# Attention on one core: pair 1's keys and queries loaded in halves, two more output pairs stored whole

## The chip, the cores and the metric

The kernel runs on one NeuronCore of one Trainium2 chip. TensorE (PE in the profile) multiplies matrices and transposes, ScalarE (ACT) computes the exponentials, VectorE (DVE) and GpSimd (POOL) do the elementwise work, and SyncE (SP) issues nearly all transfers between device memory and the on-chip memory SBUF. Sixteen DMA engines carry every transfer. The metric is the device time of one execution in microseconds (us). The kernel before takes 114.5 us, the median of three runs from 113.86 to 114.7.

## The reference

Attention over 64 independent heads (8 batches of 8), each with 512 rows of 64 numbers:

```
scores = einsum('bhqd,bhkd->bhqk', q, k) * (1 / sqrt(64))
scores = scores - scores.max(axis=-1, keepdims=True)
attn = exp(scores);  attn = attn / attn.sum(axis=-1, keepdims=True)
out = einsum('bhqk,bhkd->bhqd', attn, v)        # all float32, (8, 8, 512, 64)
```

Each of q, k, v and the output is 8 MB. A head of one of them is 128 KB. The kernel works on fp16 copies, subtracts one constant instead of each row's maximum, and gets the sum of a row from a column of ones beside the values.

## The kernel before

**Tiling.** The 64 heads are taken as 32 pairs, numbered 0 to 31, each with a head 0 and a head 1. (g,h) below is head h of pair g. A row of the SBUF tile of one pair holds four rows of each head, so that one partition reads 1 KB in one piece from each head.

**The way of one pair.** Its k, q and v are loaded in one transfer of 256 KB each (`load`, L488), cast to fp16 (`cast`: keys and queries at L504, values at L494, all on GpSimd; for queries of pair 1 alone VectorE casts one half at L502 and GpSimd the other at L503). Eight transposes on TensorE (L535) and a copy on VectorE (L548; for pair 1 two copies at L542) give the layout that the scores need. Score matmuls (L575) fill a PSUM tile of 128x1024, and ScalarE takes its exponential in one instruction (L579). For 16 of the tiles VectorE computes the exponential with bit operations instead (L599 and L616 to L639), which gives two tiles, pe and pd, that the value matmuls (L680) add up. The first pair has code of its own (`first_pair`, L729), with its k and q loaded head by head, on two queues (L722, L723).

**Output.** A unit is 128 query rows of one head; four units make a head. VectorE normalises up to seven units at once (reciprocal L645, product L650) into a ring of 112 units, and `store` sends a head, 128 KB, to memory (L670). Heads are numbered in the ring in the order in which their values are computed, from unit 4 on; (8,0) has units 68 to 71, (8,1) 72 to 75, (10,0) 84 to 87, (10,1) 88 to 91. The first product writes three units, 4 to 6, and product number n + 1 writes units 7n to 7n + 6, so unit u is overwritten by the product that writes unit u + 112, which has to wait until the store of unit u has landed. For the pairs in `PAIRED` (3 and 13) head 0's turn issues nothing, and head 1's turn issues one transfer of 256 KB for both (L668).

**Order.** A planner (`Plan`) walks through an estimated time line before the kernel is built and writes one list of steps. Every engine gets its instructions in the order of this list; semaphores make each wait for its data. The list does not depend on `PAIRED`. First SP issues the first pair's q, then 21 loads in this order: keys 1, queries 1, keys 2, queries 2, values 0, keys and queries 3, keys and queries 4, keys and queries 5, values 1, and so on to keys and queries 7. Keys, queries and values each have seven buffers, so the loads of later pairs wait for casts of earlier ones. Late in the list, loads and stores alternate on SP's queue. Around the change it reads: stores (6,0), (6,1); keys and queries 29; stores (8,0), (8,1); keys and queries 30; values 28 and 26; store (9,0); keys and queries 31; stores (9,1), (10,0); values 29 and 27; stores (10,1), (11,0).

**Waits of transfers.** Each transfer reports its end on one of eight semaphores, taken in turn by all queues. A transfer is issued when the one that had its semaphore before, eight places earlier, has landed.

Of the kernel before, what the change touches and what calls it, by code (L numbers as in the profile page):

```python
# [17 lines left out]
class Plan:  # L18
# [25 lines left out]
    SCALE_PORT, PRODUCT_PORT, GAP, REACH = 271, 537, 20, 5  # L44
    FIRST_LAND, LOAD, STORE, LATENCY, ISSUE = 5200, 740, 370, 2300, 470
    QUEUED, URGENT = 3500, 16
    PAIRED = (3, 13)
    RAW, QK16, NV, NU = 7, 5, 12, 112
    PAIR, DUEK, DUEV, DUEL, PRE = 3300, 2800, 4000, 7000, 0

# [357 lines left out]
def kernel(  # L408
# [7 lines left out]
    nc = tc.nc  # L416
# [50 lines left out]
    def source(src, g):  # L467
        b, h = g // ppb, 2 * (g % ppb)
        return src[b, h : h + 2].rearrange("h (p i) d -> p h i d", i=NI)

    def load_tile(g, name):
        t = lpool.tile(
            [P, 2, NI, D],
            FP32,
            tag=f"{name}32",
            name=f"{name}32_{g}",
            bufs=7,
        )
        raw.setdefault(g, {})[name] = t
        return t  # L480

    def load(g, names):
        if g >= NP:
            return
        for name in names:
            src = {"q": q, "k": k, "v": v}[name]
            t = load_tile(g, name)
            nc.sync.dma_start(out=t[:, :, :, :], in_=source(src, g))  # L488

    def cast(g, name):  # L490
# [167 lines left out]
    def store():  # L658
# [4 lines left out]
        u = u0 % NU  # L663
        if g in Plan.PAIRED and h == 0:
            return
        if g in Plan.PAIRED:
            both = ring[:, u - NI : u + NI, :].rearrange("p (h i) d -> p h i d", h=2)
# [149 lines left out]
    with tc.manual_schedule():  # L817
        plan = Plan(groups, NP, 3)
        steps = plan.run()
        first_loads()  # L820
        for g, name in plan.first_loads:
            load(g, name)
        make_identity(nc, ident)
        for n in range(NV):
            nc.vector.memset(vps[n][:, :, :, D : D + 1], 1.0)
        first_pair()
        do = {
            "transposes": transposes,
            "scores": scores,
            "values": values,  # L830
            "load": load,
            "store": store,
            "cast": cast_behind,
            "raise": raise_,
            "copy": lambda g, b: copy(g),
            "pass": pass_,
            "last": last_values,
            "finish": finish,
            "rec": lambda u, n, b: reciprocal(u, n),
            "mul": lambda u, n, b: normalise(u, n),  # L840
        }
        for what, *args in steps:
            do[what](*args)
# [30 lines left out]
```

## Time and profile before

| | us |
|---|---|
| median of three runs | 114.5 (113.86 to 114.7) |
| profiled execution, whole | 114.31 |
| its span, first to last instruction | 112.5 |
| TensorE busy | 104.0 |
| VectorE busy | 101.3 |
| ScalarE busy | 105.6 |
| GpSimd busy | 65.2 |

In one line of the groups stand the line of the kernel, the engine, the operation, what is written from what, the shapes and the count; behind the first bar the busy time and the mean duration of one in ns; behind the second the idle time of the engine ahead of these instructions and what ended it. A line of the timeline has the start in us, the duration in us, the engine and what it does; in brackets stands the idle time before it. Instructions that follow one another are merged, with their count. SPq is SP's queue of transfers. A line of the transfers has the size of one and the median time from issue to landing. A line of a table of windows has the stretch, its length, the busy time of each engine with its count, TensorE's granted clock, the share of time in which the DMA engines were busy, and GB/s. The share can be a little over 1, since packets overlap.

### The profile page before, as it was taken

Reading aid. Unit: us, or ns where it says so; the run is one execution under the profiler, and the core shown is the slowest. Engines: PE = TensorE matmul, PEld = TensorE weight load, DVE = VectorE, ACT = ScalarE, POOL = GpSimd, SP = SyncE. Lnnn points to the kernel's source line nnn. Section 1 sums busy time; section 2 is a strip of 40 time slices with the busy share of each in tenths; the row PEclk is TensorE's granted clock in tenths of the full one; section 3 lists DMA queues with packets and bytes.
Section 4 is the critical chain, followed back from the end, with each engine's and each line's share of the span. In section 5 each row is a group of like instructions: output and inputs, shape, how many; then the busy total and the mean of one; then the engine's idle time right before and its main releaser. Section 6 shows DMA issues by size and latency. Waiting matters only on the chain.

```text
span 112.5 us, 4427 instructions
## 1 busy us (share of the span) xinstructions
PE 104.0 (92%) x1731; PEld 71.1 (63%) x1731; DVE 101.3 (90%) x226; ACT 105.6 (94%) x118; POOL 65.2 (58%) x127
## 2 busy tenths in 40 slices
PE   7988889899999998999999999999999999999970
PEld 7654546576775564657677557678667765776560
DVE  1547999999989999999999999999999999999760
ACT  4689999999999999999999999999999999999960
POOL 2166788265478866686847888755868796000000
PEclk9999999999999999999999999999999999999999
DMA  2999999999999999999999999999997976848435
GB/s 90 271 340 354 346 349 349 342 349 348 348 329 331 344 350 347 344 353 325 283 299 376 346 312 363 358 374 353 357 305 229 289 244 212 270 143 268 159 99 184
DMA packets 35349, 33.84 MB, mean 301 GB/s; under 512 B 2560, under 2 KB 35328, under 8 KB 35328
## 3 DMA queue, kind: packets, MB, share of 16 engines
q1 hardware_dynamic: 34752, 33.04, 90.8%
q10 hardware_dynamic: 576, 0.52, 1.4%
q8 instruction: 13, 0.21, 0.8%
q14 instruction: 8, 0.07, 0.2%
HBM read 25.17 MB, written 8.39 MB: 298 GB/s over the span
## 4 chain that ended last, share of the span: by engine, by line
DVE 45%; PE 42%; ACT 7%; issue 2%; DMA 1%
PE o L680 18%; PE st L575 14%; DVE pd L599 10%; DVE tqk L548 8%; DVE ring L650 8%; ACT pt L579 7%; PE tp L535 6%; DVE m L633 4%; DVE pd L639 3%; PE st_0a L727 3%; DVE pe L625 3%; DVE m L616 2%; DVE m L635 2%; DVE rc L645 2%; DMA out_dram<-ring 1%
## 5 line engine op out<-in xcount | busy, mean ns | idle before, releaser
L579 ACT ACTIVATE pt<-st 128x1024 f16<-128x1024 f32 (+1 forms) x110 | 100.3, 1114 | 0.0
L680 PEld LDWEIGHTS <-pt 128*128 128x128 f16 x880 | 38.9, 98 | 12.3 <-issue 10.6
L680 PE MATMUL o<-vp,pt 128*128 128x65 f16 x880 | 46.3, 194 | 0.2
L575 PE MATMUL st<-tqk 64*128 64x512 f16 (+1 forms) x250 | 42.4, 381 | 2.9 <-ACT pt L579 1.7
L504 POOL CAST qkp<-k 128x512 f16<-128x512 f32 x31 | 21.5, 692 | 12.2 <-DMA k<-in_k_dram 5.2
L494 POOL CAST vp<-v 128x512 f16<-128x512 f32 x32 | 21.8, 695 | 7.7 <-DVE rc L645 2.6
L504 POOL CAST qkp<-q 128x512 f16<-128x512 f32 x30 | 21.1, 703 | 6.6 <-DVE rc L645 2.2
L650 DVE TENSOR_TENSOR ring<-o,rc 128x448 f32<-128x448 f32 (+2 forms) x37 | 22.3, 606 | 0.6
L680 PE MATMUL o<-vp,pe 128*128 128x65 f16 x128 | 22.1, 195 | 0.0
L680 PE MATMUL o<-vp,pd 128*128 128x65 f16 x128 | 21.9, 193 | 0.0
L548 DVE COPY tqk<-tp 128x1024 f16<-128x1024 f16 x30 | 20.3, 677 | 0.2 <-PE tp L535 0.2
L535 PE MATMUL tp<-ident,qkp 128*128 128x128 f16 x248 | 19.5, 219 | 0.9 <-DVE ring L650 0.7
L599 DVE TENSOR_SCALAR pd<-st 128x1024 uint16<-128x1024 f32 x16 | 19.5, 1217 | 0.7 <-PE st L575 0.7
L575 PEld LDWEIGHTS <-tqk 64*128 64x128 f16 x250 | 11.7, 93 | 12.3 <-issue 4.8
L535 PEld LDWEIGHTS <-qkp 128*128 128x128 f16 x248 | 14.3, 97 | 7.3 <-issue 4.4
L680 PEld LDWEIGHTS <-pe 128*128 128x128 f16 x128 | 12.5, 97 | 3.8 <-issue 2.9
L680 PEld LDWEIGHTS <-pd 128*128 128x128 f16 x128 | 12.5, 98 | 0.0
L639 DVE TENSOR_TENSOR pd<-pd,m 128x1024 f16<-128x1024 f16 x16 | 10.9, 682 | 0.0
L633 DVE TENSOR_TENSOR m<-m 128x1024 f16<-128x1024 f16 x16 | 10.9, 681 | 0.0
L645 DVE RECIPROCAL rc<-o 128x7 f32<-128x7 f32 (+2 forms) x37 | 7.2, 195 | 1.9 <-PE o L680 1.9
L625 DVE TENSOR_SCALAR pe<-pd 128x1024 uint16<-128x1024 uint16 x16 | 6.8, 425 | 0.0
L635 DVE TENSOR_SCALAR m<-m 128x1024 f16<-128x1024 f16 x16 | 6.5, 409 | 0.0
(50 smaller groups left out, 36.6 us busy)
## 6 DMA issues: line engine op xcount, KB each, us to landing
v<-in_v_dram SPq DMA_DIRECT2D x32, 256.0 KB, 5.8
k<-in_k_dram SPq DMA_DIRECT2D x31, 256.0 KB, 5.9
q<-in_q_dram SPq DMA_DIRECT2D x31, 256.0 KB, 5.9
out_dram<-ring SPq DMA_DIRECT2D x57, 128.0 KB, 3.7
out_dram<-ring SPq DMA_DIRECT2D x2, 256.0 KB, 3.3
k<-in_k_dram ACTq DMA_DIRECT2D x2, 128.0 KB, 2.9
q<-in_q_dram SPq DMA_DIRECT2D x2, 128.0 KB, 2.7
out_dram<-ring ACTq DMA_DIRECT2D x2, 128.0 KB, 2.0
```

What stands on the lines that cost most here:

```text
L494: return nc.gpsimd.tensor_copy(out=vps[g % NV][:, :, :, 0:D], in_=raw[g]["v"][:, :, :, :])
L504: return nc.gpsimd.tensor_copy(out=dst, in_=src[:, :, :, :])
L535: reads[g] = nc.tensor.transpose(tps[g][:, n, i, :], qkp[g][:, n, i, :], ident)
L548: nc.vector.tensor_copy(out=tqk[g][:, :, :], in_=tps.pop(g).rearrange("p n i c -> p n (i c)"))
L575: nc.tensor.matmul(st[:, x, cols], kc, qc[:, cols], start=True, stop=True)
L579: nc.scalar.activation(out=pt[:, :, cols], in_=st[:, :, cols], func=EXP, scale=scale, bias=SHIFT)
L599: nc.vector.tensor_scalar(out=r["pd"][:, :, :], in0=r["st"][:, :, :], scalar1=BITS, scalar2=BIAS, op0=AluOp.mult, op1=AluOp.add,)
L625: ins = nc.vector.tensor_scalar(out=r["pe"][:, :, :], in0=u[:, :, :], scalar1=0x7C00, scalar2=None, op0=AluOp.bitwise_and,)
L633: ins = nc.vector.tensor_tensor(out=m16, in0=m16, in1=m16, op=AluOp.mult)
L639: ins = nc.vector.tensor_tensor(out=u16, in0=u16, in1=m16, op=AluOp.mult)
L650: nc.vector.tensor_tensor(out=ring[:, u % NU : u % NU + n, :], in0=o[:, x : x + n, 0:D], in1=rcs.pop(u)[:, 0:n].broadcast_to([P, n, D]), o ...
L680: nc.tensor.matmul(os[u // 7][:, u % 7, :], part[:, y * P : (y + 1) * P], vps[g % NV][:, h, c, :], start=(n == 0), stop=(n == len(parts) - 1),
```

## The change

Two edits. In `load`, the keys and the queries of pair 1 are read with two transfers of 128 KB each, one for each head, instead of one of 256 KB. The casts are as before: keys 1 in one instruction for both heads, queries 1 in two, each of which reads both heads. In `PAIRED` the pairs 8 and 10 are added: their head 0 is no longer stored in its own turn, and the turn of head 1 stores both heads in one transfer. Two transfers are added and two taken away.

```
-    PAIRED = (3, 13)
+    PAIRED = (3, 8, 10, 13)
...
             src = {"q": q, "k": k, "v": v}[name]
             t = load_tile(g, name)
+            if g == 1 and name != "v":
+                for h in range(2):
+                    nc.sync.dma_start(out=t[:, h], in_=source(src, g)[:, h])
+                continue
             nc.sync.dma_start(out=t[:, :, :, :], in_=source(src, g))
```

## The prediction

> **What bounds the kernel now.** I read the busy table first, then the exponentials' row among the groups, then ScalarE's own timeline.
>
> ```profile
> PE 104.0 (92%) x1731; PEld 71.1 (63%) x1731; DVE 101.3 (90%) x226; ACT 105.6 (94%) x118; POOL 65.2 (58%) x127
> ...
> L579 ACT ACTIVATE pt<-st 128x1024 f16<-128x1024 f32 (+1 forms) x110 | 100.3, 1114 | 0.0
> ```
>
> ```profile
> 7.43 1.02 ACT L777 ACTIVATE pt<-st 128x1024 f16<-128x1024 f32 x1 [0.28 <-PE st L770]
> 8.35 100.29 ACT L579 ACTIVATE pt<-st 128x1024 f16<-128x1024 f32 x110
> ```
>
> Three engines are over 90% busy, so the shares alone do not decide. The next row does: the 110 exponentials of L579 have 0.0 us of idle time ahead of them. They run from 8.35 to 108.64 without a gap that the profile counts. The span of 112.5 us is therefore 8.35 us of start, 100.29 us of exponentials and 3.9 us of last values, last normalisation and last store. A change moves the time if it delays the first exponentials, opens a gap in this row, lengthens or shortens its steps, or moves the tail.
>
> The steps have a little play. In one quiet stretch, in one slow one and at the end ScalarE's timeline reads:
>
> ```profile
> 45.98 2.93 ACT L579 ACTIVATE pt<-st 128x1024 f16<-128x1024 f32 x3
> ...
> 88.93 3.15 ACT L579 ACTIVATE pt<-st 128x1024 f16<-128x1024 f32 x3
> ...
> 107.42 1.22 ACT L579 ACTIVATE pt<-st 128x512 f16<-128x512 f32 x2
> ```
>
> Taking 1.11 us for the last of the three, the first row has (2.93 - 1.11) / 2 = 0.91 us from start to start, the second 1.02. At 0.91 throughout, 108 whole steps and the two half ones of the third row take 98.3 + 1.2 = 99.5 us against 100.29. So all that any better feeding of ScalarE could win is about 0.8 us.
>
> **The start, where the loads change.** The chain that ended last runs through pair 1's transposes and their copies here:
>
> ```profile
> 7.61 0.34 PE tp L535 x4
> 7.97 0.77 DVE tqk L542 x2
> ```
>
> Pair 1's transposes (tp) stand on it, its casts and its loads do not. The timelines of SP, GpSimd and TensorE show why:
>
> ```profile
> 0.75 0.86 SPq L723 DMA_DIRECT2D q<-in_q_dram  x2
> 1.66 0.43 SPq L488 DMA_DIRECT2D k<-in_k_dram  x1
> 2.12 0.47 SPq L488 DMA_DIRECT2D q<-in_q_dram  x1
> 2.64 0.47 SPq L488 DMA_DIRECT2D k<-in_k_dram  x1
> ...
> 6.09 0.37 SPq L488 DMA_DIRECT2D q<-in_q_dram  x1
> 7.00 0.37 SPq L488 DMA_DIRECT2D k<-in_k_dram  x1
> ```
>
> ```profile
> 6.13 0.61 POOL L504 CAST qkp<-k 128x512 f16<-128x512 f32 x1 [2.27 <-DMA k<-in_k_dram]
> 7.04 0.52 POOL L503 CAST qkp<-q 128x256 f16<-128x256 f32 x1 [0.29 <-DMA q<-in_q_dram]
> 7.79 0.61 POOL L504 CAST qkp<-k 128x512 f16<-128x512 f32 x1 [0.22 <-DMA k<-in_k_dram]
> ...
> 9.29 0.62 POOL L494 CAST vp<-v 128x512 f16<-128x512 f32 x1
> ```
>
> ```profile
> 7.23 0.38 PE L575 MATMUL st<-qt,kt 64*128 64x512 f16 x2
> 7.54 0.62 PE L535 MATMUL tp<-ident,qkp 128*128 128x128 f16 x8
> 8.79 1.03 PE L575 MATMUL st<-tqk 64*128 64x512 f16 x6 [0.63 <-DVE tqk L542]
> ...
> 10.20 0.42 PE L680 MATMUL o<-vp,pt 128*128 128x65 f16 x8
> ```
>
> **Issue.** Two transfers go, four come. In the first row SP issues two of 128 KB in 0.86 us and is free for the next at 1.66, so one costs (1.66 - 0.75) / 2 = 0.455 us. Four start at 1.66, 2.12, 2.57 and 3.03, and pair 2's keys follow at 3.48 instead of 2.64: all later first loads are issued 0.84 us later, until SP waits for landings anyway. That is soon: each transfer from the ninth on waits for the one eight places before it. The thirteenth (queries 4) starts at 6.09, when the fifth (keys 1) lands, as its cast at 6.13 shows; the fourteenth at 7.00, as the sixth does. From there SP is paced by landings, and the lost 0.84 us are gone if the landings keep their times.
>
> **Landing of keys and queries 1.** It isn't shown for halves behind a backlog, so I bound it. Late end: the last half is issued at 3.03 instead of 2.12, and the whole 0.91 us reaches the landing, 7.9. Early end: it lands as the first pair's halves did, 2.7 us after issue, at 5.7.
>
> ```profile
> k<-in_k_dram SPq DMA_DIRECT2D x31, 256.0 KB, 5.9
> ...
> k<-in_k_dram ACTq DMA_DIRECT2D x2, 128.0 KB, 2.9
> q<-in_q_dram SPq DMA_DIRECT2D x2, 128.0 KB, 2.7
> ```
>
> ```profile
> 3.50:4.50 1.00, 1.00 (x14) 0.89 (x11) 0.64 (x5) 0.58 (x3) 0.36 (x1) 1.00 0.70 196
> 4.50:5.50 1.00, 1.00 (x9) 0.34 (x7) 0.61 (x3) 0.68 (x3) 0.00 (x0) 1.00 0.99 281
> 72.00:82.00 10.00, 9.99 (x184) 6.95 (x181) 9.97 (x24) 10.00 (x12) 6.87 (x14) 1.00 1.07 359
> ```
>
> The last two columns of these windows are the DMA share and the GB/s. Full is 1.07, as in the last row. At the start there is a dip to 0.70 for a microsecond, then they fill again. Where they are full, a landing is set by the bytes ahead of it, and these are the same 1 MB. I take the unchanged landing, about 7.0.
>
> **What hides either end.** An earlier landing buys nothing on the chain: the transposes at 7.54 come straight behind the matmuls of 7.23, which are pair 0's last scores. A later one has a cover. The eight transposes start (0.62 - 0.22) / 7 = 0.057 us apart (0.22 is one, from their group's mean of 219 ns), so the seventh, the first to need GpSimd's half of queries 1, starts at 7.88, while that half ends at 7.56: 0.3 us. ScalarE asks for pair 1's first scores 0.91 after 8.35, at 9.26; they end at 8.79 + 0.39 = 9.18: 0.1 us more at best. Past some 0.3 us, every delay is a gap in ScalarE's row. The late end thus costs 0.91 - 0.3 = 0.6 us. Values 0, cast at 9.29 to 9.91, have another 0.3 us until 10.20. I book 0 for the start, between 0 and +0.6.
>
> ```profile
> L535 PE MATMUL tp<-ident,qkp 128*128 128x128 f16 x248 | 19.5, 219 | 0.9 <-DVE ring L650 0.7
> ```
>
> **The added waits.** Keys 1's cast, and both halves of queries 1's, now need two transfers each: three more waits, at most. Behind them stand, on GpSimd, the casts of pair 2, and on VectorE the copies of pair 1's transposes. A wait instruction of its own takes
>
> ```profile
> L650 DVEq EVENT_SEMAPHORE  x21: 21/49/50, 62.8 to 108.5; - x21
> ```
>
> 0.05 us, which the 0.3 us hide. Zero; 0.1 us if that cover is gone.
>
> **The two stores.** In the order list the stores of (8,0) and (8,1) are the two of 72.19 below, (10,0) is the second of 78.10, and (10,1) the first of 80.95.
>
> ```profile
> 72.19 1.02 SPq L670 DMA_DIRECT2D out_dram<-ring  x2
> ...
> 78.10 0.93 SPq L670 DMA_DIRECT2D out_dram<-ring  x2
> 79.50 1.13 SPq L488 DMA_DIRECT2D v<-in_v_dram  x2
> 80.95 0.83 SPq L670 DMA_DIRECT2D out_dram<-ring  x2
> ```
>
> ```profile
> out_dram<-ring SPq DMA_DIRECT2D x57, 128.0 KB, 3.7
> out_dram<-ring SPq DMA_DIRECT2D x2, 256.0 KB, 3.3
> ```
>
> Two issues of about 0.46 us leave SP; the loads behind them (values 29 and 27 at 79.50 among them) come up to that much earlier. The bytes are the same, and from 72 to 82 the DMA engines are full (1.07), so little lands earlier; what does feeds work behind an uninterrupted ScalarE. Gain: 0, and at most the 0.8 us of play above. The cost would be in the ring: head (8,0) leaves with (8,1), and (10,0) with (10,1). Units 68 and 84 are written again 112 units later, by the normalisations of units 175 to 181 and 196 to 202:
>
> ```profile
> 84.40 0.62 DVE L650 TENSOR_TENSOR ring<-o,rc 128x448 f32<-128x448 f32 x1
> ...
> 91.08 0.62 DVE L650 TENSOR_TENSOR ring<-o,rc 128x448 f32<-128x448 f32 x1
> ```
>
> With 72.8 + 3.7 and 80.95 + 3.7 the data are out by 76.5 and 84.7: 8 and 6 us before. Hidden; only a store twice as late would cost anything. The tail keeps its last instructions and their waits: 0.
>
> **Sum.** 114.31 us for the profiled execution (112.5 of span and 1.8 around it), plus 0 + 0 + 0. That execution lies 0.2 us under the median of the runs, 114.5, and inside their spread of 0.84 us; with no change in the sum I forecast the median, **114.5**.
>
> **Rivals.** (1) *Slower: the loads come late.* If the issue, not the bytes, sets the landings (the dip to 0.70 says that some engines ran dry once already), queries 1 land up to 0.9 us later, the transposes' cover is used up, and ScalarE has one gap of up to 0.6 us at 9.26 that nothing gives back: 115.1. It decides from 7.3 us on for that landing. Against it: the DMA engines are near full again from 4.5 us on (0.99), and the halves of the first pair needed only 2.7 us. Chance 0.2.
>
> The Trainium skill, DMA: Bandwidth & Descriptors, section Rules for kernel authors, speaks against splitting (coalesce many small transfers into one), and its section on the anatomy of a DMA puts about 2.0 us of fixed cost on each. Paid one after the other, two more transfers would be 4 us by that page's figure, an estimate; the trace has loads of 5.9 us starting 0.75 us apart, so the fixed part overlaps here, and the sum does without it.
>
> (2) *Faster: the halves fill the dip.* If the smaller transfers reach all engines sooner, the dip of 3.5 to 5.5 (1.07 - 0.70 and 1.07 - 0.99, together 0.45 us of full rate) closes, the whole load stream runs up to 0.45 us earlier, and the casts that follow landings (7.79) with it. At most that 0.45 us comes out of the slow steps of ScalarE: 114.05. For it: GpSimd's waits for loads. Against it: ScalarE has no idle time, and pair 1's transposes cannot start earlier. Chance 0.25.
>
> (3) *The change does nothing that it says*: both casts still wait for both heads, so nothing starts on one head alone. That is part of the forecast, 114.5, which has 0.5. The remaining 0.05 is for effects of shifted transfers that I have no row for.
>
> **How the numbers follow.** A median of this kernel moves by about half the spread of its runs, 0.4 us, and 1% (1.15 us) is about what a measurement can tell from no change. Low end: 114.05 - 0.4 = 113.6. High end: 115.1 + 0.4 = 115.5. Beyond 1% on the slow side needs rival (1) at its full price and a bad draw, 0.09; on the fast side more than all play in ScalarE's row, 0.05; within 1%, 0.86.
>
> **What would show it.** In the changed profile: four half loads at about 1.66, 2.1, 2.6 and 3.0 and keys 2 near 3.5; the casts of pair 1 starting at 6.1 or earlier and at 7.0, give or take 0.2; L579 again with 0.0 idle and 8.35 as its start; SP without an issue between the stores of (6,1) and (8,1) other than loads; no wait of VectorE on a store. I am wrong if a gap stands before ScalarE's second exponential of L579, if queries 1 land past 7.3, or if the total of L579 moves by more than 0.8 us.

## The result, and the profile after

Timed side by side, 22 runs each, the kernel after takes 114.54 us (114.14 to 115.5) and the kernel before 114.19. The ratio is 1.0036, with a 95% interval from 1.0020 to 1.0052: the change costs about 0.35 us, between 0.2 and 0.6. Medians here are over all executions; ratios and intervals leave out the few that were more than 1.5% slower than the fastest of their kernel. The change is small, but it is not the "no change" of the forecast. The predicted figure, 114.5, lies beside the measured one by luck: the three runs of before that it started from had a median 0.3 us above that of the 22.

The profiled execution of after took 114.8 us, with a span of 113.0. First the busy table of its page and the row of the exponentials (L583 now; the lines behind the edit have moved by 4).

```profile
PE 103.8 (92%) x1731; PEld 70.8 (63%) x1731; DVE 101.4 (90%) x226; ACT 105.7 (93%) x118; POOL 65.4 (58%) x127
...
L583 ACT ACTIVATE pt<-st 128x1024 f16<-128x1024 f32 (+1 forms) x110 | 100.5, 1102 | 0.8 <-PE st L579 0.8
```

The work is the same; the idle time ahead of the exponentials has gone from 0.0 to 0.8 us, and TensorE's scores end it. ScalarE's timeline of after says where.

```profile
7.80 2.89 ACT L583 ACTIVATE pt<-st 128x1024 f16<-128x1024 f32 x3
11.52 97.58 ACT L583 ACTIVATE pt<-st 128x1024 f16<-128x1024 f32 x107 [0.83 <-PE st L579]
```

It is one gap, ahead of the fourth of them, the exponential of tile 7. At the steps of 0.90 us that undisturbed stretches have, it was due at 7.80 + 3 x 0.90 = 10.50, and it starts at 11.52: 1.0 us is lost. All of it isn't net: this execution started the row at 7.80, 0.55 us before the 8.35 of before, for a reason that has nothing to do with the change (last section). 1.0 - 0.55 is 0.45 us, which with the span's 112.5 to 113.0 agrees. From the exponential of tile 7 on the row takes 97.58 us in after; in before, where that exponential starts at 11.06, it takes 108.64 - 11.06 = 97.58 as well. So nothing behind the gap has to be explained.

The chain that ended last, in the kernel after, from 4 us on (start, us, what):

```profile
4.01 0.47 SPq L492
4.48 0.04 issue
4.52 5.50 DMA v<-in_v_dram
10.02 0.05 issue
10.07 0.62 POOL vp L498
10.70 0.04 issue
10.74 0.41 PE o L684 x8
11.16 0.32 PE st L579 x2
```

In before the chain ran here through pair 1's transposes and none of the loads behind the first pair's; now it goes back through the load of values 0 into SP's issues. The timelines of SP, GpSimd and TensorE in the kernel after give each step:

```profile
1.64 0.90 SPq L490 DMA_DIRECT2D k<-in_k_dram  x2
2.58 0.91 SPq L490 DMA_DIRECT2D q<-in_q_dram  x2
3.54 0.43 SPq L492 DMA_DIRECT2D k<-in_k_dram  x1
4.01 0.47 SPq L492 DMA_DIRECT2D q<-in_q_dram  x1
4.52 0.47 SPq L492 DMA_DIRECT2D v<-in_v_dram  x1
```

```profile
6.01 0.61 POOL L508 CAST qkp<-k 128x512 f16<-128x512 f32 x1 [2.30 <-DMA k<-in_k_dram]
6.75 0.53 POOL L507 CAST qkp<-q 128x256 f16<-128x256 f32 x1
7.58 0.61 POOL L508 CAST qkp<-k 128x512 f16<-128x512 f32 x1 [0.30 <-DMA k<-in_k_dram]
9.31 0.61 POOL L508 CAST qkp<-q 128x512 f16<-128x512 f32 x1 [1.12 <-DMA q<-in_q_dram]
10.07 0.62 POOL L498 CAST vp<-v 128x512 f16<-128x512 f32 x1
```

```profile
9.24 0.40 PE L539 MATMUL tp<-ident,qkp 128*128 128x128 f16 x4
9.98 0.40 PE L539 MATMUL tp<-ident,qkp 128*128 128x128 f16 x4 [0.35 <-POOL qkp L508]
10.74 0.41 PE L684 MATMUL o<-vp,pt 128*128 128x65 f16 x8 [0.36 <-POOL vp L498]
11.09 0.39 PE L579 MATMUL st<-tqk 64*128 64x512 f16 x2
```

Keys 2 are issued at 3.54, 0.90 us later than before. Pair 1's halves are cast at 6.01 and 6.75, where the whole loads were cast at 6.13 and 7.04, and keys 2 at 7.58 (7.79 before); shifts of this size are within what one execution differs from the next (last section). The next two whole loads are late: queries 2 are cast at 9.31, which was 8.54, and values 0 at 10.07, which was 9.29. TensorE works in the order of the list, and the first values (L684) stand ahead of the scores of tile 7 (11.09). So ScalarE, which needs these scores, waits for a load that it doesn't use yet.

What the slower issue does to the transfers is in the windows (the last two columns are the DMA share and GB/s), first of after, then of before:

```profile
6.50:7.50 1.00, 1.00 (x12) 0.45 (x8) 0.47 (x2) 1.00 (x2) 0.65 (x2) 1.00 0.95 290
```

```profile
6.50:7.50 1.00, 0.78 (x8) 0.21 (x6) 0.74 (x3) 0.72 (x2) 0.70 (x2) 1.00 1.06 343
```

While queries 2 and values 0 should arrive, the DMA engines move 290 GB/s in place of 343.

The stores in SP's timeline of after:

```profile
72.30 0.83 SPq L674 DMA_DIRECT2D out_dram<-ring  x2
...
74.42 0.40 SPq L672 DMA_DIRECT2D out_dram<-ring  x1
...
84.01 0.42 SPq L672 DMA_DIRECT2D out_dram<-ring  x1
```

Pair 8 leaves in one transfer at 74.42 and lands 6.9 us later, at 81.3; pair 10 leaves at 84.01 and lands 4.4 us later, at 88.4. Their units are overwritten from VectorE's products at 84.87 and 91.55 on:

```profile
84.87 0.62 DVE L654 TENSOR_TENSOR ring<-o,rc 128x448 f32<-128x448 f32 x1
...
91.55 0.62 DVE L654 TENSOR_TENSOR ring<-o,rc 128x448 f32<-128x448 f32 x1
```

Neither product has idle time in front of it: no wait for a store, with 3.5 and 3.1 us to spare.

### The profile page after: what moved, and what is told of

The parts are those of the page before. It is cut to its first block, busy times and chain, and to the rows that moved or that the text cites. A ratio compares the mean times of both kernels' runs of the same rounds, so it can differ in the third digit from the quotient of the medians.

```text
span 113.0 us, 4429 instructions
## 1 busy us (share of the span) xinstructions
PE 103.8 (92%) x1731; PEld 70.8 (63%) x1731; DVE 101.4 (90%) x226; ACT 105.7 (93%) x118; POOL 65.4 (58%) x127
## 4 chain that ended last, share of the span: by engine, by line
DVE 39%; PE 37%; DMA 9%; ACT 7%; SPq 3%; issue 2%; POOL 1%; DVEq 0%
PE o L684 18%; PE st L579 13%; DVE pd L603 8%; DVE tqk L552 8%; DVE ring L654 8%; ACT pt L583 7%; PE tp L539 5%; DMA v<-in_v_dram 5%; DMA out_dram<-ring 4%; DVE m L637 4%; DVE pd L643 3%; DVE m L620 2%; DVE pe L629 2%; DVE m L639 2%; DVE rc L649 2%
## 5 line engine op out<-in xcount | busy, mean ns | idle before, releaser
L583 ACT ACTIVATE pt<-st 128x1024 f16<-128x1024 f32 (+1 forms) x110 | 100.5, 1102 | 0.8 <-PE st L579 0.8
L684 PEld LDWEIGHTS <-pt 128*128 128x128 f16 x880 | 38.9, 98 | 12.9 <-issue 11.2
L684 PE MATMUL o<-vp,pt 128*128 128x65 f16 x880 | 46.3, 194 | 0.5 <-POOL vp L498 0.4
L579 PE MATMUL st<-tqk 64*128 64x512 f16 (+1 forms) x250 | 42.4, 381 | 2.7 <-ACT pt L583 2.0
L684 PE MATMUL o<-vp,pe 128*128 128x65 f16 x128 | 22.1, 195 | 0.0
L684 PE MATMUL o<-vp,pd 128*128 128x65 f16 x128 | 21.9, 193 | 0.0
L579 PEld LDWEIGHTS <-tqk 64*128 64x128 f16 x250 | 11.6, 93 | 11.9 <-issue 4.5
L684 PEld LDWEIGHTS <-pe 128*128 128x128 f16 x128 | 12.5, 97 | 3.8 <-issue 2.9
L684 PEld LDWEIGHTS <-pd 128*128 128x128 f16 x128 | 12.5, 98 | 0.0
```

What stands on the lines that cost most here:

```text
L579: nc.tensor.matmul(st[:, x, cols], kc, qc[:, cols], start=True, stop=True)
L583: nc.scalar.activation(out=pt[:, :, cols], in_=st[:, :, cols], func=EXP, scale=scale, bias=SHIFT)
L684: nc.tensor.matmul(os[u // 7][:, u % 7, :], part[:, y * P : (y + 1) * P], vps[g % NV][:, h, c, :], start=(n == 0), stop=(n == len(parts) - 1),
```

## The experiments

The theory (A): SP needs 0.45 us for every transfer it issues, two more transfers ahead of queries 2 and values 0 make these late, and the fixed order of TensorE turns that into one gap before tile 7. Its rivals: the halves themselves, by their size, slow the queue; the cost is in the stores; or the gap is a draw of one execution. A fourth rival, that the added transfers use up two of the eight semaphores and so make SP wait, is answered by SP's rows above: up to values 0 at 4.52, and on to keys 5 at 7.08, each issue starts 0.04 to 0.07 us after the end of the one before, so no landing holds up the loads that matter. All ratios below are to the kernel before, timed beside it, with 95% intervals.

**The halved loads alone, and the two stores alone.** Run e1_loads has the edit in `load` and `PAIRED = (3, 13)`; run e2_stores has only

```
-    PAIRED = (3, 13)
+    PAIRED = (3, 8, 10, 13)
```

> The halved loads of pair 1 alone, with the stores as before. Theory A (issue): the four halves cost SP two more issues, keys 2 start 0.85-0.9 us later, queries 2 and values 0 land 0.8 us later (near 9.3 and 10.0 instead of 8.5 and 9.2), TensorE waits for their casts, and ScalarE has one gap near 11.5 us: ratio 1.003 to 1.004, the whole loss. Rival B (the halves as such spread badly over the DMA engines): the same here. Rival C (the stores): 1.000, no gap near 11.5 us.

> The two added whole-pair stores alone, loads as before. Theories A and B: ratio 1.000 (within 0.002), values 0 cast at 9.2-9.4 us, no gap in ScalarE's row. Rival C: 1.003 to 1.004.

The loads alone take 114.67 us, 1.0046 (1.0009 to 1.0082). The stores alone take 114.30, 1.0007 (0.9991 to 1.0024). The intervals just overlap; the profiles put the loss with the loads. GpSimd and ScalarE in the loads-alone kernel:

```profile
8.57 0.62 POOL L508 CAST qkp<-q 128x512 f16<-128x512 f32 x1 [0.58 <-DMA q<-in_q_dram]
9.55 0.62 POOL L498 CAST vp<-v 128x512 f16<-128x512 f32 x1 [0.37 <-DMA v<-in_v_dram]
```

```profile
7.71 2.89 ACT L583 ACTIVATE pt<-st 128x1024 f16<-128x1024 f32 x3
11.01 3.77 ACT L583 ACTIVATE pt<-st 128x1024 f16<-128x1024 f32 x4 [0.41 <-PE st L579]
```

The same gap at the same tile, smaller: values 0 come at 9.55 here and 10.07 in after. In the stores-alone kernel, whose row of exponentials starts at 8.01, nearly as early, the cast of values 0 is on time, and its page shows no gap:

```profile
9.21 0.62 POOL L494 CAST vp<-v 128x512 f16<-128x512 f32 x1
```

```profile
L579 ACT ACTIVATE pt<-st 128x1024 f16<-128x1024 f32 (+1 forms) x110 | 100.5, 1097 | 0.0
```

By the distances of after (values 0.05 us behind the cast, tile 7 another 0.78 on) tile 7 could start at 9.83 + 0.83 = 10.66, and it was due at 8.01 + 3 x 0.90 = 10.71: just in time. A start at 7.80 would have left a gap of 0.2 even so; the rest of after's 1.0 is the lateness of values 0.

**SP's time without the halves.** Runs e3_two_small and e5_four_small are the kernel before with two and with four added loads of 4 KB into tiles that nobody reads, issued right behind queries 1 (nothing of the computation is left out):

```
+        small = [cpool.tile([16, D], FP32, name=f"small{n}") for n in range(2)]
...
+            if (g, name) == (1, "q"):
+                for n in range(2):
+                    nc.sync.dma_start(out=small[n][:, :], in_=q[0, n, 0:16, :])
```

> Loads and stores as before, but behind the load of queries 1 SP issues two more loads of 4 KB each that nobody reads: two more issues, two more turns of the eight semaphores, no halves and 8 KB more. Theory A: keys 2 start 0.8-0.9 us later, values 0 are cast near 10.0 us and ScalarE has the gap: ratio 1.003 to 1.004, as with the halves. Rival B: the landings of queries 2 and values 0 stay at 8.5 and 9.2, ratio 1.000.

> As the run with two small loads behind queries 1, but four of them: SP reaches keys 2 some 1.8 us later than before the change instead of 0.9. Theory A (SP's issue time alone starves the load stream): queries 2 and values 0 land 1 us or more late (values 0 cast past 10 us), ScalarE's gap before its exponential of tile 7 is about 1 us, ratio 1.007 to 1.010, more than twice that of two. Rival B (the halves themselves spread badly, the added issues cost little): ratio below 1.004.

Two small loads: 114.42 us, 1.0029 (1.0008 to 1.0051). Four: 115.46, 1.0122 (1.0077 to 1.0168), more than expected. They add next to no bytes and split no load, so issue time ahead of the whole loads is enough for a loss of the size of the change's, and it grows with the number of issues; by the medians more than in proportion, which the intervals do not settle. SP, the window behind it, GpSimd and TensorE in the kernel with four:

```profile
2.63 1.85 SPq L826 DMA_DIRECT2D small<-in_q_dram  x4
4.53 0.42 SPq L488 DMA_DIRECT2D k<-in_k_dram  x1
```

```profile
5.50:6.50 1.00, 1.00 (x10) 0.79 (x9) 0.14 (x1) 1.00 (x3) 0.85 (x2) 1.00 0.70 176
```

```profile
9.91 0.62 POOL L494 CAST vp<-v 128x512 f16<-128x512 f32 x1 [1.06 <-DMA v<-in_v_dram]
```

```profile
10.58 0.41 PE L680 MATMUL o<-vp,pt 128*128 128x65 f16 x8 [0.18 <-POOL vp L494]
```

1.85 us without a whole load, and a microsecond follows in which the transfers fall to 176 GB/s (309 in before). Two misses belong here. In the one profile of the kernel with four, the fastest of its six executions (114.87 us), the gap of about 1 us that was expected isn't there: the row starts at 8.38, tile 7 was due at 8.38 + 3 x 0.90 = 11.08 and starts at 11.36, behind the first values, so 0.3 us are lost at the expected place. In the one profile of the kernel with two, values 0 are cast at 9.28, on time, and there is no gap, although the transfers are as thin as in after (298 GB/s from 6.5 to 7.5). Its runs show a loss that this execution (114.2 us, among the fastest of its twelve) doesn't have, so where they lose it isn't shown by a row.

**The halves without SP's time.** Run e4_pool_queue has the halved loads with queries 1 issued from GpSimd's queue, and the identity of the transposes made ahead of them:

```
+                    queue = nc.gpsimd if name == "q" else nc.sync
+                    queue.dma_start(out=t[:, h], in_=source(src, g)[:, h])
```

> Keys 1 in halves on SP's queue, queries 1 in halves on GpSimd's own queue, which is idle from 1.3 to 3.5 us; stores as before. SP issues two transfers for pair 1 as before, so keys 2 start near 2.6 us. Theory A: values 0 are cast at 9.3 us or earlier, no gap near 11.5 us, ratio 1.000 or below as long as queries 1 land by 7.3 us (if they land at 8 us, a gap of 0.6 us near 9.3 us and 1.004). Rival B: the halves still cost, 1.003.

114.65 us, 1.0045 (1.0014 to 1.0076): no better. But the place is another one. GpSimd, ScalarE and one window in this kernel:

```profile
7.02 0.62 POOL L509 CAST qkp<-k 128x512 f16<-128x512 f32 x1 [3.24 <-DMA k<-in_k_dram]
...
9.18 0.62 POOL L499 CAST vp<-v 128x512 f16<-128x512 f32 x1
```

```profile
8.12 1.02 ACT L584 ACTIVATE pt<-st 128x1024 f16<-128x1024 f32 x1
9.37 5.61 ACT L584 ACTIVATE pt<-st 128x1024 f16<-128x1024 f32 x6 [0.23 <-PE st L580]
```

```profile
6.50:7.50 1.00, 0.61 (x4) 0.11 (x4) 0.51 (x3) 0.87 (x2) 0.48 (x1) 1.00 1.04 354
```

With SP free for keys 2 after two issues, as in before, values 0 are on time (9.18), the window from 6.5 to 7.5 is full again (354 GB/s), and tile 7 has no gap, as the theory says. Keys 1 are now cast a microsecond later than in after, and the gap is the one of the prediction's rival (1): before the second exponential, at 9.37, through pair 1's transposes. This execution traded one late load for another, and the run doesn't tell what the halves would cost in a queue that delays nobody.

**Keys alone in halves.** Run e6_keys_only splits keys 1 and leaves queries 1 whole (`if g == 1 and name == "k":`): one more transfer instead of two.

> Only keys 1 in halves, queries 1 whole, stores as before: SP loses one issue, 0.45 us. Theory A: values 0 land about 0.3 us late, which is the cover that the first values have, so ratio 1.000 to 1.002. Rival B: the share of the halves stays, about half of 1.0046, ratio 1.002 to 1.003, and the DMA rate from 3.5 to 4.5 us is below that of the kernel before.

114.38 us, 1.0013 (0.9989 to 1.0037). It lies between none and two, as a loss per issue would have it, but the interval holds both ends. The transfers from 3.5 to 4.5 us are not below those of before (216 GB/s against 196), as they would be if halves as such spread badly.

**TensorE's order.** If the first values stand in the way of tile 7's scores, moving these scores ahead of them must give time back. Run e7_swap does that to the kernel before, run e8_swap_halves to the kernel after:

```
+        first_values = next(n for n, x in enumerate(steps) if x[0] == "values")
+        steps.insert(first_values, steps.pop(steps.index(("scores", 7, False))))
```

> The kernel before with one step moved: the scores of tile 7 stand ahead of the first two units of values on TensorE, instead of behind them. Values 0 are in time here, so the move should change nothing in either theory: ratio 0.999 to 1.001. It is the base for the next run.

> The whole change and the same moved step. If ScalarE's gap comes from tile 7's scores standing behind the first values on TensorE, which wait for late values 0 (theory A and B alike in where the loss arises), the gap before its exponential of tile 7 is 0.2 us or less, the ratio falls from 1.0036 to 1.000 to 1.001 and the slower start of the stream costs nothing. If the loss arises elsewhere (rival: pair 2's transposes, or the whole stream being late up to 18 us), the ratio stays at 1.003 to 1.004.

In before the move is worth nothing: 114.19 us, 0.9996 (0.9967 to 1.0024). In after it gives 114.30, 1.0010 (0.9984 to 1.0036). GpSimd and ScalarE of that kernel:

```profile
9.23 0.61 POOL L508 CAST qkp<-q 128x512 f16<-128x512 f32 x1 [1.12 <-DMA q<-in_q_dram]
9.98 0.62 POOL L498 CAST vp<-v 128x512 f16<-128x512 f32 x1
```

```profile
8.40 6.52 ACT L583 ACTIVATE pt<-st 128x1024 f16<-128x1024 f32 x7
```

The loads are as late as in after (9.23 and 9.98 against 9.31 and 10.07), and ScalarE runs through tile 7 without a gap. Part of that is this execution's late start, 8.40, 0.6 us behind that of after. In the old order tile 7 would have started 0.78 us after the first values, as in after (11.52 - 10.74), so at 10.65 + 0.78 = 11.43, and it was due at 8.40 + 3 x 0.90 = 11.10: by this estimate the move spared 0.3 us here.

**The pair again, and two variants.** On another chip: the kernel after (e9_change_again), the kernel after with the move (e10_swap_halves_again), the move with four small loads (e11_swap_four_small), and the move with keys alone in halves (e12_swap_keys).

> The whole change once more, on the same chip as the next three. Both theories: 1.002 to 1.005, and a second profile of where ScalarE waits: theory A says before its exponential of tile 7, with values 0 cast past 9.5 us.

> The whole change with tile 7's scores ahead of the first values, once more beside the whole change without it. Theory A: 0.2 to 0.4 us below the change, 1.000 to 1.001 of the kernel before. Rival (the loss is not at tile 7): the same time as the change.

> Four small loads behind queries 1 and the moved step, the same mechanism at a size that is well clear of the noise. Without the moved step the four cost 1.0122. Theory A: values 0 still come at 10 us, but one exponential of 0.9 us more is fed before TensorE waits for them, so 0.6 to 0.9 us less: 1.004 to 1.007. Rival: 1.011 to 1.013 as before.

> Keys 1 in halves, queries 1 whole, stores as before, and the moved step: the version with the least delay and the most cover. Theory A: 0.999 to 1.000; a gain over the kernel before would need the earlier keys 1 to start ScalarE earlier, which pair 0's matmuls do not allow. Rival: 1.001 to 1.002, as without the moved step.

| kernel | us | ratio to before |
|---|---|---|
| after | 114.52 | 1.0037 (1.0011 to 1.0062) |
| after with the move | 114.32 | 1.0022 (0.9999 to 1.0045) |
| move, four small loads | 115.40 | 1.0101 (1.0059 to 1.0144) |
| move, keys 1 in halves | 114.30 | 1.0018 (1.0000 to 1.0037) |

The loss repeats. Its profiled execution, at 116.2 us the slowest of its runs, has the gap at tile 7 again, with values 0 cast at 10.46; the size of that gap is not used here. The move, at 1.0022, missed the 1.000 to 1.001 that was expected, and on this chip alone the kernels with and without it can't be told apart, since their intervals overlap nearly whole. With the runs of all calls taken together, 33 of after and 23 of after with the move, after is 1.0019 times as long (1.0006 to 1.0031, by resampling the medians); 22 of the 33 come from the first call, beside which no run with the move stands, but the median of before was 114.2 in each. By that, about 0.2 of the 0.35 us hang on tile 7's scores standing behind the first values. The rest, some 0.13 us, remains with the move (1.0011, 1.0001 to 1.0018), and its place isn't shown.

Four small loads with the move missed what was expected: they cost as much as without it, within the intervals. TensorE and ScalarE of that kernel say why:

```profile
13.95 0.40 PE L535 MATMUL tp<-ident,qkp 128*128 128x128 f16 x4 [0.93 <-POOL qkp L504]
```

```profile
14.83 1.94 ACT L579 ACTIVATE pt<-st 128x1024 f16<-128x1024 f32 x2 [0.85 <-PE st L575]
```

With twice the delay the next load is late as well: TensorE waits for the cast of queries 3 in the middle of pair 3's transposes, and ScalarE has its gap three tiles further on. The move protects one tile, not the ones behind.

The move with keys 1 in halves came out at the rival's expectation, 1.001 to 1.002, and not at the theory's 0.999 to 1.000. ScalarE in its profile:

```profile
7.68 1.04 ACT L583 ACTIVATE pt<-st 128x1024 f16<-128x1024 f32 x1
9.18 5.61 ACT L583 ACTIVATE pt<-st 128x1024 f16<-128x1024 f32 x6 [0.46 <-PE st L579]
```

The row starts early here, at 7.68, and the gap stands before the second exponential, where rival (1) of the prediction had it: TensorE waits 0.43 us, in the middle of pair 1's transposes, for the cast of queries 1 that VectorE starts at 7.34 (7.01 in before). The profile of keys alone without the move has 0.2 us there: its second exponential starts at 9.14, and 8.02 + 0.90 = 8.92 was due.

**All profiles together.** Values 0 are cast at 9.21, 9.29 and 9.73 in the three profiles with pair 1's loads as in before (stores alone, before, before with the move). With keys and queries 1 in halves they are cast at 9.55, 9.57, 9.98 and 10.07, leaving out the execution of 116.2 us; with two small loads at 9.28, with four at 9.91 and 10.47. So single landings overlap, and the delay of one execution, 0.78 us in after, is not the delay of all. The transfers part more clearly: from 6.5 to 7.5 us the first three profiles move 342 to 349 GB/s, the four with halves 259 to 290, two small loads 298, and the halves with SP undelayed 354; with four small loads the thin stretch is 5.5 to 6.5, at 176 and 151 (309 to 329 in the first three). A thinner stream of transfers goes with SP's delay, with or without halves.

None of these kernels is faster than the kernel before.

**Open.** Whether the halves cost something beyond the two issues: 1.0046 with halves and 1.0029 with small loads have overlapping intervals, and the one run meant to separate them changed the queue as well. How much of the loss stands at tile 7: of the profiles with added issues ahead of the whole loads, some show the gap there, those with keys 1 alone in halves lose time before the second exponential, and one shows none. Why the loss of the kernel with two small loads is absent from its profile. And where the 0.13 us are that the move leaves.

## Why the prediction was wrong

**What bounds the kernel**: right. ScalarE's row of exponentials sets the time, and in the profile of after the loss is one gap in it. The prediction named three signs that would make it wrong. The third came true if it is read from the row's start to its end, 109.10 - 7.80 = 101.3 us against 100.29; the busy total, 100.5 against 100.3, did not move. The first two looked at the wrong place: there is no gap before the second exponential, and queries 1 don't land past 7.3.

**Issue**: here the prediction failed. Its first half held: halves at 1.64, 2.11, 2.58 and 3.06, and the next five loads 0.86 to 0.90 us later (0.84 predicted). SP had also caught up at keys 5 (7.08 against 7.00). But the step's conclusion, that "the lost 0.84 us are gone if the landings keep their times", failed, since its condition did not hold. The landings of the whole loads behind the halves did not keep their times. In after, values 0 are issued at 4.52 and cast at 10.07, 0.78 us later than before, so nearly the whole delay came through in this execution; in the others with halves it was 0.26 to 0.69. The assumption rested on full DMA engines, where only bytes count. But they were full because SP had issued ahead: with SP 0.9 us later they fall to 290 GB/s between 6.5 and 7.5 (343 in before), and with four small loads to 176 a microsecond earlier. With SP undelayed (e4) that window stays full, at 354.

The Trainium skill, DMA: Bandwidth & Descriptors, section Issuing engines are not separate DMA queues, calls the time to start a transfer usually small relative to the transfer itself. Measured, it is 0.45 us against 5.9, so small it is; it decides here all the same, because in a start-up with one issuing queue it adds up ahead of every load behind it. The 2.0 us of fixed cost that the prediction quotes stand in a section on transfers issued from GpSimd; on SP's queue four added transfers cost 1.3 us in all here, less than the 1.85 us of their issue.

**Landing of keys and queries 1**: about the unchanged landing, as taken. With queries 1 in halves on SP's queue GpSimd's cast comes at 6.68 to 6.82 us in four executions; with queries 1 whole and issued at 2.12 it comes between 6.19 and 7.47 in six. The Trainium skill, Perfetto Trace Analysis, section DMA Optimizations, says that splitting may let some transfers start sooner, and that the whole task may end sooner if the DMA engines are generally idle. No run here shows an earlier landing clear of the differences between executions, and these engines are not idle (share 0.91 and more from 4.5 us on in after); the unsplit loads behind are the ones that paid.

**What hides either end**: the step gave values 0 a cover of 0.3 us up to 10.20 but looked for lateness at queries 1 only, and booked 0. Put in the measured 0.78, and 0.78 - 0.3 = 0.5 us is what it would have given for that execution, against the 0.45 net that the profiles show. The cover was in the list; the delay to set against it was left at zero.

**The added waits, the two stores, the tail**: right. The stores alone give 1.0007, and no product waits for a store. The two whole-pair stores needed 6.9 and 4.4 us instead of the 3.7 used, and pair 10's was issued at 84.01, 3 us later than the 80.95 reckoned with, so the margins were 3.5 and 3.1 us and not 8 and 6. From tile 7 on ScalarE loses no more time than before.

**The rivals**: rival (1) had the right kind of mechanism, with issue and not bytes setting the landings, and one gap that nothing gives back. Place and price were off: tile 7 at 11.5 through values 0, not 9.26 through queries 1, and 0.35 us, not 0.6. Its own place appeared only where keys 1 or queries 1 came late in another way (e4, e6, e12). Of rival (2) nothing is seen: the dip did not close (DMA share 0.61 from 3.5 to 4.5 us, 0.70 in before), and no earlier landing of the halves is shown.

## What to carry to other kernels

In a start-up where one queue issues all loads, cost a split not at the split load but at the loads behind it: multiply the added issues by the time of one, and follow each later load to its first reader. "The DMA engines are full, so only bytes count" held here only as long as the issuing engine stayed ahead; look at what a later issue does to the windows that follow. And where one engine works in a fixed order, a late operand stops the work queued behind its reader as well, so its slack is that of the nearest starving engine. A single profile can show the place of a loss; where landings and starts differ by more than the effect from one execution to the next, its size comes from many runs.

## What the runs showed of the hardware beside that

**TensorE runs at half pace at first, while its granted clock reads 1.00** (in the windows of these three kernels from 2.5 us on). Pair 0's last four query transposes, in TensorE's timelines of before, of after, and of after with the move:

```profile
5.67 0.61 PE L765 MATMUL tp_qb<-ident,q 128*128 128x128 f16 x4
```

```profile
5.24 0.40 PE L769 MATMUL tp_qb<-ident,q 128*128 128x128 f16 x4
```

```profile
5.73 0.61 PE L769 MATMUL tp_qb<-ident,q 128*128 128x128 f16 x4
```

The same four instructions take 0.61 us in some executions and 0.40 in others; single ones start 0.106 us apart in the first case and 0.057 in the second. That moves ScalarE's start by up to about half a microsecond, with and without the change (some 0.1 us of the difference between before and after is there already at the first transposes, 3.63 and 3.53, behind the first loads): its row of L579 starts at 8.35 in before and 8.01 in the stores-alone kernel, its row of L583 at 7.80 in after and 8.40 in after with the move. Single spans mix this with the change, and only the many runs part them. The Trainium skill, TensorE: Matmul & The Clock Gate, section Part 1: The HAM clock gate, gives 106 to 107 ns from matmul to matmul cold and 55 to 56 warm, with a change-over that varies from run to run because its window runs freely; the spacings here agree.

**The same load lands up to 1.3 us apart.** Keys 1, whole and issued from SP at 1.65 or 1.66, are cast as they land, at 5.43, 5.56, 5.91, 6.11, 6.13 and 6.74 us in six executions (four small loads, stores alone, two small loads, four small loads with the move, before, before with the move). In halves they are cast between 5.66 and 6.22 us with SP's queue alone.

**GpSimd's queue was no free second queue here.** With queries 1 issued there, from 1.44 us on where after issues them from 2.58, keys 1, issued from SP at the same time as in after, were cast at 7.02 instead of 6.01. GpSimd's two issues took 0.54 and 0.68 us against SP's 0.43. One run; why keys 1 came late was not tried.
